# The bidirectional recurrence of a two-block transformer: preparation without GpSimd, two products per chunk in the chain

## The chip, the cores and the metric

One core of a Trainium2 chip. The metric is the device time of one execution, in microseconds, median of three runs. The kernel is written with a tile scheduler: the program lists instructions with their data, the scheduler decides in which order each engine gets them, and each engine works off its own queue in that order.

## The reference

Two blocks of two layers each over a sequence of 256 latent tokens (and 256 context tokens in the first block), width 1024. The first block's layers mix tokens in three ways at once, from one input projection: neighbourhood attention (512 columns), a bidirectional RWKV-7 recurrence (256 columns, 4 heads of 64) and a conformer convolution (256 columns). Layer 0 then has a feed-forward part, layer 1 a mixture of 8 experts of which each token takes two. The second block has block attention, spatial gating, a convolution and a feed-forward part. The recurrence is what the change is about:

```python
def _rwkv7_scan(r, w, k, v, z, b):
    def step(S, inp):
        r_t, w_t, k_t, v_t, z_t, b_t = inp
        s_z = jnp.einsum('ghvk,ghk->ghv', S, z_t)
        S = S * w_t[:, :, None, :] + s_z[..., None] * b_t[:, :, None, :] + v_t[..., None] * k_t[:, :, None, :]
        return S, jnp.einsum('ghvk,ghk->ghv', S, r_t)
    _, y = lax.scan(step, jnp.zeros((G, H, dh, dh), jnp.float32), (r, w, k, v, z, b))
    return y
...
    kk = kk * lax.rsqrt(jnp.sum(kk * kk, axis=-1, keepdims=True) + 1e-12)
...
        a = jax.nn.sigmoid(a0[d] + ad @ a2[d])
        kd = heads(k * (1.0 + (a - 1.0) * k_a))
        per_dir.append((heads(decay), kd, kk * heads(a), g))
```

z is −kk, b is kk·a, w the decay; the second direction runs over the reversed tokens. T is 512 (context, then latent). Layer 1 needs only the latent tokens' outputs.

## The kernel before

Weights are read from HBM as float32 and split into a high part (`wh`, a cast on ScalarE, L182) and a low part (`wl`, a subtraction, L183, on VectorE or GpSimd); each projection is three matmuls. `mixer()` builds one layer's mixing from generators: `prep` (p), `conv` (x), `gram` (g), `inverse` (i), `near` (n: projections of q, k and v of the neighbourhood attention), `chain` (c), `attend` (a), `taps` (t) and a few more. The string SEQ[layer] (L51 to L54) gives the order in which their steps are written down, a letter a step. For x and n the letter's case sets the engine of `wl`: lower case GpSimd, upper case VectorE. Each generator has PSUM banks of its own by tag: three for the recurrence's preparation, gram and inverse, four for near, one each for the chain's two directions.

The recurrence is done in 8 chunks of 64 tokens. The index `dh` is direction and pair of heads (four values, called heads here); the two heads of a pair lie in the partition halves 0 to 63 and 64 to 127.

- `prep`, per dh: ee and aa are sigmoids (a tanh on ScalarE, L519, and an affine pass on GpSimd, L520). A scan over ee (L624) gives cs, two exponentials the decays LAM and il (L626, L627). kd (L629, L630) and `ka` (L631, GpSimd) are multiplied by il into BK: two products 64x512 on VectorE and two on GpSimd (the loop of L632, products L634 and L635). kkn and r times LAM are ZR (L636, L637). `sqk` (L639) is the operand of the bonus.
- `gram`: masked products of BK and ZR give S for all chunks.
- `inverse`: of the triangular part, first on VectorE a solve of 32x32 blocks by rows (transposes Ad, L686; products and sums, L696 and L698, into Xi), then transposes of Xi into TD and TN (L704, L706), then on TensorE products with TN, copied to Gs, and with Gs, copied into TD.
- `near` multiplies the tokens with the q, k and v weights: 192 matmuls of 512 columns and 192 of 256 columns (for v) in layer 0, half of q in layer 1. They write PSUM tiles, and ScalarE copies these to q, k and v.
- `chain`: per chunk `ready` turns v (identity products, L776 copies them into UV) and BK (transposes, L785 copies them, scaled, into BT). Then S·UV and ZR·PP are summed and copied to RH (L802), TD·RH is copied into UV (L810), BT·UV and the state PP make the next PP (L821 to L824). Last comes the output py (L835 copies it into ZR).

Every matmul is written at L154, every transpose at L158; the profile tells them apart by tile: `psprep`, `psgram`, `psinv`, `psnap` (near), `pschain`.

## Time and profile before

| | |
|---|---|
| runs | 2874.79, 2882.23, 2890.8 us; median 2882.23 |
| the profiled execution | 2886.99 us, its span 2885.2 us |
| TensorE busy | 2750.6 us, 95% of the span; granted clock 0.965 on average |
| VectorE, ScalarE, GpSimd busy | 1988.4 (69%), 1468.3 (51%), 348.5 us (12%) |

The first block's two layers take some 2,300 us of the span, 1,060 of them the experts. In layer 0 the preparation of the recurrence starts at 96.7 us, gram ends at 169.8, inverse and near projections at 260.4, the chain (with attention between) at 361.9. In layer 1 the same points are about 940, 1009, 1071 and 1165. Times are read from the span's start. A row of the timeline is an instruction, or a few of a kind (xN); what stands in brackets is the engine's idle time before it, and the instruction that ended it. A busy time of TensorE counts overlapping matmuls once; rows overlap, so that the distance of two starts is what one costs. The clock column is the granted clock of TensorE, 1.00 being 2.4 GHz.

### The profile page before, as it was taken

The page shows a single profiled execution, that of the slowest core. Times are in us where ns is not written, and L with a number is a line of the kernel's source. Part 1 is how long each engine was busy: PE and PEld are TensorE (multiplying, and loading weights), DVE is VectorE, ACT ScalarE, POOL GpSimd, SP SyncE. Part 2 cuts the span into 40 slices and gives each one's busy share as a digit, 9 for nine tenths or more (in the row PEclk, how much of TensorE's full clock was granted, in tenths as well). Part 3 has the DMA queues.
Part 4 walks back from the last instruction along what each step waited for, and adds up shares of the span by engine and source line. Part 5 has one row for each costly group of instructions (what it writes and reads, how often), then busy time and mean ns, then how long its engine had stood idle before and what let it go on. Part 6 is the DMA issues. An engine that isn't in the chain of part 4 may idle for free. (4 is left out here: it accounts for less than half of the span.)

```text
span 2885.2 us, 42860 instructions
## 1 busy us (share of the span) xinstructions
PE 2750.6 (95%) x17006; PEld 2257.8 (78%) x17006; DVE 1988.4 (69%) x2753; ACT 1468.3 (51%) x2032; POOL 348.5 (12%) x256
## 2 busy tenths in 40 slices
PE   6998999999998879999989999999999999999999
PEld 4677656778886766677867777778777889998999
DVE  4685474322225796488878888888889868856784
ACT  3313243322224332477757777767777646644563
POOL 1420012211001610100000000000000221301120
PEclk9898799999999998999999999999999999999999
DMA  6122155333333224579988999899989835553453
GB/s 227 51 74 74 52 150 193 96 123 94 97 99 105 81 88 140 173 293 352 319 321 325 322 353 344 328 338 362 337 325 349 307 114 175 183 183 117 161 184 109
DMA packets 108098, 585.77 MB, mean 203 GB/s; under 512 B 12657, under 2 KB 19825, under 8 KB 54129
## 3 DMA queue, kind: packets, MB, share of 16 engines
q1 hardware_dynamic: 107888, 582.95, 57.5%
q8 instruction: 136, 2.23, 0.3%
q14 instruction: 74, 0.60, 0.1%
HBM read 580.80 MB, written 2.10 MB: 202 GB/s over the span
## 5 line engine op out<-in xcount | busy, mean ns | idle before, releaser
L183 DVE TENSOR_TENSOR wl<-wr,wh 128x1024 fp32r<-128x1024 f32 x978 | 1169.5, 1225 | 477.9 <-ACT wh L182 465.6
L182 ACT CAST wh<-wr 128x1024 fp32r<-128x1024 f32 x992 | 1003.8, 1044 | 681.1 <-PE psffn L154 193.2
L154 PE MATMUL psmoe<-wh,xH 128*128 128x512 f32 x896 | 354.9, 397 | 3.4 <-ACT wh L182 3.4
L154 PE MATMUL psmoe<-wl,xH 128*128 128x512 f32 x896 | 356.2, 398 | 1.0 <-DVE wl L183 0.7
L154 PE MATMUL psmoe<-wh,xL 128*128 128x512 f32 x896 | 355.5, 397 | 0.0
L154 PEld LDWEIGHTS psmoe<-wl,xH 128*128 128x128 f32 x896 | 168.3, 188 | 45.6 <-DVE wl L183 6.5
L154 PEld LDWEIGHTS psmoe<-wh,xH 128*128 128x128 f32 x896 | 168.4, 188 | 44.4 <-ACT wh L182 5.0
L154 PE MATMUL pssf<-oh,wl 128*128 128x256 f32 x704 | 199.5, 284 | 0.0
L154 PE MATMUL pssf<-ohT,wh 128*128 128x256 f32 x704 | 199.2, 284 | 0.0
L154 PEld LDWEIGHTS psmoe<-wh,xL 128*128 128x128 f32 x896 | 168.4, 188 | 39.1
L154 PE MATMUL pssf<-oh,wh 128*128 128x256 f32 x704 | 198.9, 284 | 0.0
L154 PE MATMUL psmoe<-wh,aL 128*128 128x512 f32 x448 | 178.3, 398 | 2.0 <-DVE aL L183 2.0
L154 PE MATMUL psmoe<-wh,aH 128*128 128x512 f32 x448 | 175.6, 397 | 2.5 <-ACT aH L182 2.5
L154 PE MATMUL psmoe<-wl,aH 128*128 128x512 f32 x448 | 163.3, 400 | 0.0
L1551 POOL TENSOR_SCALAR x<-x,fin 128x256 f32<-128x256 f32 x8 | 12.2, 1542 | 1057.5 <-DMA wr<-w_in 1057.3
L154 PE MATMUL psffn<-h2L,wh 128*128 128x512 f32 x352 | 138.7, 394 | 1.3 <-POOL h2L L257 1.3
L154 PE MATMUL psffn<-h2H,wh 128*128 128x512 f32 x352 | 138.2, 395 | 1.0 <-ACT h2H L256 1.0
L154 PE MATMUL psffn<-h2H,wl 128*128 128x512 f32 x352 | 137.5, 392 | 0.0
L154 PEld LDWEIGHTS pssf<-oh,wl 128*128 128x128 f32 x704 | 135.2, 192 | 0.0
L154 PEld LDWEIGHTS pssf<-ohT,wh 128*128 128x128 f32 x704 | 135.1, 192 | 0.0
L154 PEld LDWEIGHTS pssf<-oh,wh 128*128 128x128 f32 x704 | 135.0, 192 | 0.0
L154 PEld LDWEIGHTS psmoe<-wh,aL 128*128 128x128 f32 x448 | 84.2, 188 | 24.4 <-DVE aL L183 4.4
(476 smaller groups left out, 5624.6 us busy)
## 6 DMA issues: line engine op xcount, KB each, us to landing
wr<-moe_w_gate SPq DMA_DIRECT2D x112, 1024.0 KB, 7.0
wr<-moe_w_up SPq DMA_DIRECT2D x112, 1024.0 KB, 6.6
wr<-moe_w_down SPq DMA_DIRECT2D x112, 1024.0 KB, 7.0
wm<-mod_w SPq DMA_DIRECT2D x96, 512.0 KB, 4.3
wr<-f_up SPq DMA_DIRECT2D x44, 1024.0 KB, 4.9
wr<-w_in SPq DMA_DIRECT2D x52, 512.0 KB, 3.8
wr<-w_in SPq DMA_DIRECT2D x16, 1024.0 KB, 5.0
wr<-f_down SPq DMA_DIRECT2D x16, 1024.0 KB, 5.0
```

The lines of the kernel that those rows point to most:

```text
L154: i = self.nc.tensor.matmul(out, lhsT, rhs, start=start, stop=stop, **kw)
L182: self.nc.scalar.copy(H, src)
L183: (eng or self.nc.vector).tensor_sub(L, src, H.bitcast(F32))
L1551: nc.gpsimd.tensor_scalar(x[:, k], x[:, k], fin[:, k:k + 1], None, op0=ALU.mult)
```

## The change

In `prep` GpSimd is left with little. The sigmoid's affine pass goes to ScalarE; aa stays a tanh, and the constants (`oka`, `hka`, and `kkh`, half of kkn) make up for it; kd's affine pass goes to ScalarE, `ka` to VectorE, and so do all four products of BK. In SEQ[0] the conv's steps are lower case (their L parts go to GpSimd), one step of near's becomes lower case, and chain steps stand between those of near's v part.

In the recurrence a new function `turned()` stands at the start of `inverse`. It turns v of all chunks (into UV, which has two places: the LAM tile, and a new one), multiplies S with them, scales BK of seven chunks in place by the decay of the chunk, transposes it and writes it back, and turns ZR by identity products. Behind each half of the inverse, TD multiplies the turned ZR. A chunk of the chain then has two dependent products: ZR·PP, added to a TD·UV that is already in the bank, copied into UV; and BK·UV, added to the scaled state. The solve's Ad, Xi and Gs no longer have a pool of their own but lie in the tile of near's v, and `self.after` asks that the second part of near's v comes behind the last TD·ZR.

```diff
-SEQ = [("pppppgggXXggggggggggggginNnniNNcactcccttatcatt...
+SEQ = [("pppppgggxxggggggggggggginNnnicNccNactcttatcatt...
...
         def sigm(dst, src, **kw):
             nc.scalar.activation(dst, src, AF.Tanh, scale=0.5, **kw)
-            nc.gpsimd.tensor_scalar(dst, dst, 0.5, 0.5, op0=ALU.mult, op1=ALU.add)
+            nc.scalar.activation(dst, dst, AF.Copy, scale=0.5, bias=0.5)
...
+                kkh = PA.tile([128, 2, 512], F32, name=self.nm("kkh"))
+                nc.scalar.activation(kkh, kkn, AF.Copy, scale=0.5)
...
-                        sigm(aa, p2, bias=hw[:, 4 + dh:5 + dh])
+                        nc.scalar.activation(aa, p2, AF.Tanh, scale=0.5, bias=hw[:, 4 + dh:5 + dh])
...
-                        nc.vector.tensor_scalar(kd, aa, P("ka", hp), oka[:, hp:hp + 1], op0=ALU.mult, op1=ALU.add)
+                        nc.scalar.activation(kd, aa, AF.Identity, scale=hka[:, hp:hp + 1], bias=oka[:, hp:hp + 1])
                         nc.vector.tensor_mul(kd, kd, kx[:, hp])
-                        nc.gpsimd.tensor_mul(ka, aa, kkn[:, hp])
-                        for ab, eng in ((0, nc.vector), (1, nc.gpsimd)):
+                        nc.vector.scalar_tensor_tensor(ka, aa, 1.0, kkh[:, hp], op0=ALU.add, op1=ALU.mult)
+                        for ab in range(2):
                             o = slice(64 * ab, 64 * ab + 64)
-                            eng.tensor_tensor(o4(BK[o, dh, :, 1 - ab]), rv(ka[o], d), il4[o], ALU.mult)
-                            eng.tensor_tensor(o4(BK[o, dh, :, ab]), rv(kd[o], d), il4[o], ALU.mult)
+                            nc.vector.tensor_tensor(o4(BK[o, dh, :, 1 - ab]), rv(ka[o], d), il4[o], ALU.mult)
+                            nc.vector.tensor_tensor(o4(BK[o, dh, :, ab]), rv(kd[o], d), il4[o], ALU.mult)
...
+        def turned():
+            nc.vector.tensor_copy(lam, LAM[:, :, :, 64])
+            UV = LAM[:, :, :, 0:64], PC.tile([128, 4, 8, 64], F32, name=self.nm("UV"))
+            for c in range(8):
+                pv = self.ps((128, 2, 2, 2, 64))
...
+                            self.mm(pv[o, 0, d, hp], (vr if d else vv)[o, hp, c * 64:c * 64 + 64], self.ident[o, o], True, True, chain=pv)
...
+                    nc.scalar.copy(UV[ab][o, :, c], pv[o, 0].rearrange("p d h t -> p (d h) t"))
...
+                            self.mm(pv[r, 1, d, hp], S[o, ab, (2 * d + hp) * 8 + c, 0:64], UV[ab][o, 2 * d + hp, c], True, True, chain=pv)
...
+                    nc.scalar.copy(UV[ab][r, :, c], pv[r, 1].rearrange("p d h t -> p (d h) t"))
...
+                    nc.scalar.activation(b, b, AF.Copy, scale=lam[:, dh, c:c + 1])
+                    self.tp(pb[:, dh].rearrange("p a t -> p (a t)"), b, self.ident, chain=pb)
+                for ab in range(2):
+                    nc.scalar.activation(BK[:, :, c, ab], pb[:, :, ab], AF.Copy, scale=self.sg[:, ab:ab + 1])
+            for dh in range(4):
...
+                        self.mm(pz[r, c], ZR[o, dh, c + 1, 0], self.ident[o, o], True, True, chain=pz)
+                nc.scalar.copy(ZR[:, dh, 1:, 0], pz)
         def inverse():
+            turned()
...
-                Ad = PI.tile([128, 32, 32], F32, name=self.nm("Ad"), tag="Ad")
-                Xi = PI.tile([128, 32, 32], F32, name=self.nm("Xi"))
+                Ad, Xi = [v[:, 2 * i:2 * i + 2].rearrange("p a b -> p (a b)").rearrange("p (a b) -> p a b", a=32) for i in range(2)]
...
-                Gs = PI.tile([128, 32, 32], F32, name=self.nm("Gs"), tag="Ad")
+                Gs = Ad
...
+                    for dh in range(2 * uh, 2 * uh + 2):
...
+                                inverted = self.mm(pz[o, c], ZR[r, dh, c + 1, 0], TD[r, dh * 8 + c + 1], True, True, chain=pz)
+                        nc.vector.tensor_copy(ZR[:, dh, 1:, 0], pz)
...
         def near():
+                if inverted is not None:
+                    self.after = inverted.ins.name
...
+            def own(d, c):
+                W = self.ps((128, 2, 2, 64), tag=f"c{d}")
...
+                            self.mm(W[o, 0, hp], BK[:, 2 * d + hp, c - 1, ab], UV[ab][:, 2 * d + hp, c - 1], True, True, chain=W)
...
+                        self.mm(W[r, 1, hp], TD[r, (2 * d + hp) * 8 + c], UV[ab][r, 2 * d + hp, c], hp == 0, c == 0 and hp == 1, chain=W)
```

What it moves. VectorE in layer 0, preparation of the second of the four heads, before (cs is the scan, `sqk` the bonus operand):

```order
L624 SCALAR_TENSOR_TENSOR cs_802<-msk_730,ee_800 128x256 x2
L629 TENSOR_SCALAR kd_804<-aa_801,prm_71,oka_208 128x512
L629 TENSOR_SCALAR kd_837<-aa_834,prm_71,oka_208 128x512
L630 TENSOR_TENSOR kd_804<-kd_804,kx_472 128x512
L634 TENSOR_TENSOR BK_462<-ka_805,il_803 64x8x64
L635 TENSOR_TENSOR BK_462<-kd_804,il_803 64x8x64
L636 TENSOR_TENSOR ZR_458<-kkn_729,LAM_463 128x8x64
L637 TENSOR_TENSOR ZR_458<-rr_471,LAM_463 128x8x64
L639 SCALAR_TENSOR_TENSOR sqk_827<-rr_471,prm_71,kd_804 128x512
```

and now:

```order
L633 SCALAR_TENSOR_TENSOR cs_805<-msk_732,ee_803 128x256 x2
L639 TENSOR_TENSOR kd_807<-kd_807,kx_474 128x512
L640 SCALAR_TENSOR_TENSOR ka_808<-aa_804,kkh_768 128x512
L645 TENSOR_TENSOR ZR_460<-kkn_731,LAM_465 128x8x64
L643 TENSOR_TENSOR BK_464<-ka_808,il_806 64x8x64
L644 TENSOR_TENSOR BK_464<-kd_807,il_806 64x8x64
L643 TENSOR_TENSOR BK_464<-ka_808,il_806 64x8x64
L644 TENSOR_TENSOR BK_464<-kd_807,il_806 64x8x64
L646 TENSOR_TENSOR ZR_460<-rr_473,LAM_465 128x8x64
L648 SCALAR_TENSOR_TENSOR sqk_829<-rr_473,prm_71,kd_807 128x512
```

Two BK rows and the `ka` row have come in; the two kd rows with scalars are gone.

TensorE in layer 0 at the end of gram, before:

```order
L154 MATMUL psgram_1120<-ZR_458,BK_462 128x128 x4
L154 MATMUL psgram_1126<-ZR_458,BK_462 128x128 x4
L154 MATMUL psnap_1277<-hH_235,wh_1267 128x512
L154 MATMUL psnap_1277<-hL_236,wh_1267 128x512
L154 MATMUL psnap_1277<-hH_235,wl_1268 128x512
```

and now, where vv and vr are v and its reverse, `cst` the identity, LAM and UV the two places of the turned v:

```order
L155 MATMUL psnap_1590<-hL_238,wh_1580 128x512
L155 MATMUL psnap_1590<-hH_237,wl_1581 128x512
L155 MATMUL psinv_1170<-cst,vv_221 64x64 x4
L155 MATMUL psinv_1170<-cst,vr_222 64x64 x3
L155 MATMUL psinv_1138<-cst,vv_221 64x64 x4
L155 MATMUL psinv_1138<-cst,vr_222 64x64 x4
L155 MATMUL psinv_1170<-cst,vr_222 64x64
L155 MATMUL psinv_1202<-cst,vv_221 64x64 x4
L155 MATMUL psinv_1202<-cst,vr_222 64x64 x4
L155 MATMUL psnap_1590<-hH_237,wh_1580 128x512
L155 MATMUL psinv_1138<-LAM_465,S_905 64x64
L155 MATMUL psinv_1138<-UV_1137,S_905 64x64
```

Before, 192 matmuls of near's follow the gram products without a break. Now the products of `turned` come first, with 11 of near's between them, and the other 181 behind. Ahead of the last 52 gram products, 30 conv products stood behind the last `sqk`; now 13 do.

TensorE in layer 1, at the first products with TN, before (here 146 products of near's v part stand ahead of them):

```order
L154 MATMUL psnap_7997<-wl_7985,hH_6500 128x256
L154 MATMUL psnap_7994<-wh_7990,hH_6500 128x256
L154 MATMUL psnap_7994<-wh_7990,hL_6501 128x256
L154 MATMUL psinv_7597<-TN_7589,S_7357 32x32
L154 MATMUL psinv_7667<-TN_7589,S_7357 32x32
```

and now, at the last products of TD and ZR, behind which 147 of near's v part stand:

```order
L155 MATMUL psnap_8362<-wl_8358,hH_6609 128x256
L155 MATMUL psinv_8188<-TD_7465,ZR_6675 64x64 x14
L155 MATMUL psinv_8204<-TD_7465,ZR_6675 64x64 x14
L155 MATMUL psnap_8361<-wh_8351,hH_6609 128x256
L155 MATMUL psnap_8361<-wh_8351,hL_6610 128x256
```

The v products that ran ahead of TN now run behind the inverse. Ahead of the gram of layer 1, 25 near products of 512 columns stood between the last lora products and the gram's last groups; now 6 do.

## Rows read from the trace of the kernel before

**Rows 1.** The page, part 1: busy time, share of the span, instructions.
```profile
PE 2750.6 (95%) x17006; PEld 2257.8 (78%) x17006; DVE 1988.4 (69%) x2753; ACT 1468.3 (51%) x2032; POOL 348.5 (12%) x256
```

**Rows 2.** Windows: stretch, length; busy PE, PEld, DVE, ACT, POOL; clock, DMA share, GB/s.
```profile
96.70:169.80 73.10, 64.42 (x298) 46.97 (x296) 50.95 (x64) 16.27 (x24) 42.05 (x26) 0.77 0.14 44
169.80:260.40 90.60, 78.91 (x643) 69.45 (x642) 64.22 (x141) 23.02 (x35) 10.76 (x4) 0.89 0.20 65
260.40:361.90 101.50, 100.48 (x1042) 70.76 (x1044) 52.96 (x131) 30.13 (x74) 0.61 (x1) 0.80 0.20 63
220.00:240.00 20.00, 14.11 (x284) 13.39 (x285) 10.57 (x6) 4.61 (x8) 0.00 (x0) 0.52 0.16 54
940.00:1009.00 69.00, 57.50 (x390) 48.54 (x388) 53.99 (x69) 21.95 (x32) 44.24 (x26) 0.90 0.27 85
1009.00:1071.00 62.00, 46.48 (x524) 42.22 (x525) 57.52 (x134) 15.65 (x26) 12.64 (x5) 0.89 0.17 52
1230.00:2290.00 1060.00, 1026.87 (x4608) 823.32 (x4607) 911.08 (x915) 758.41 (x852) 1.72 (x3) 0.99 0.90 334
```

**Rows 3.** Timeline of TensorE: start, length, instruction, idle before it and releaser.
```profile
148.87 1.75 PE L154 MATMUL psprep<-cst,sqk 128*128 128x2 f32 x8 [4.96 <-DVE sqk L639]
...
160.01 9.84 PE L154 MATMUL psgram<-ZR,BK 64*128 64x128 f32 x104
...
226.10 3.62 PE L154 MATMUL psinv<-TN,S 32*32 32x32 f32 x126 [5.84 <-DVE TN L706]
...
1057.20 0.38 PE L154 MATMUL psinv<-TN,S 32*32 32x32 f32 x4 [14.34 <-DVE TN L706]
```

**Rows 4.** Timeline of VectorE in the first layer's preparation.
```profile
111.88 0.75 DVE L607 SCALAR_TENSOR_TENSOR kkn<-kx,prm,psprep 128x512 f32<-128x512 f32 x1 [4.19 <-PE psprep L158]
...
126.05 1.76 DVE L635 TENSOR_TENSOR BK<-kd,il 64x512 f32<-64x512 f32 x1
...
134.28 0.67 DVE L634 TENSOR_TENSOR BK<-ka,il 64x512 f32<-64x512 f32 x1
134.88 0.67 DVE L635 TENSOR_TENSOR BK<-kd,il 64x512 f32<-64x512 f32 x1
...
136.74 1.25 DVE L624 TENSOR_TENSOR_SCAN cs<-msk,ee 128x256 f32<-128x256 f32 x2
...
143.50 0.68 DVE L634 TENSOR_TENSOR BK<-ka,il 64x512 f32<-64x512 f32 x1 [3.79 <-POOL ka L631]
...
148.08 0.74 DVE L639 SCALAR_TENSOR_TENSOR sqk<-rr,prm,kd 128x512 f32<-128x512 f32 x1
```

**Rows 5.** Timeline of GpSimd in the same stretch.
```profile
134.04 6.82 POOL L634 TENSOR_TENSOR BK<-ka,il 64x512 f32<-64x512 f32 x1 [3.05 <-ACT il L627]
```

**Rows 6.** Timeline of TensorE in the first layer's chain.
```profile
260.38 0.45 PE L154 MATMUL pschain<-cst,vv 64*64 64x64 f32 x8
...
262.38 0.66 PE L158 MATMUL pschain<-cst,BK 128*128 128x128 f32 x4 [0.26 <-ACT UV L776]
262.97 0.68 PE L154 MATMUL pschain<-UV,S 64*64 64x64 f32 x16
```

**Rows 7.** ScalarE in that chain: two rows of its timeline, one group by line.
```profile
261.58 0.74 ACT L776 COPY UV<-pschain 64x256 f32<-64x256 f32 x2
...
263.89 0.84 ACT L785 ACTIVATE BT<-pschain,cst 128x256 f32<-128x256 f32 x2
...
L876 ACT COPY q<-psatt 128x128 f32<-128x128 f32 x3 | 0.8, 265 | 4.4 <-PE psatt L154 4.4
```

**Rows 8.** Timeline of TensorE, near products: first and last of 25, and of 40.
```profile
170.12 0.40 PE L154 MATMUL psnap<-hL,wh 128*128 128x512 f32 x1
...
175.58 0.39 PE L154 MATMUL psnap<-hL,wh 128*128 128x512 f32 x1
...
1038.04 0.28 PE L154 MATMUL psnap<-wh,hL 128*128 128x256 f32 x1
...
1042.59 0.28 PE L154 MATMUL psnap<-wh,hL 128*128 128x256 f32 x1
```

More of the change, by code (lines that the diff above doesn't have):

```diff
@@ L144, in __init__ @@
         self.last = {}
+        self.after = None
         self.n = 0
@@ L154, in mm @@
         i = self.nc.tensor.matmul(out, lhsT, rhs, start=start, stop=stop, **kw)
+        if self.after is not None:
+            self.tc.add_manual_dep(i.ins, self.after, NOSYNC, reason="the order of two stages")
+            self.after = None
         return self._chain(i, chain)
@@ L484, in mixer @@
         oka = P0.tile([128, 2], F32, name=self.nm("oka"))
-        nc.vector.tensor_scalar(oka, P("ka", 0, 2), -1.0, 1.0, op0=ALU.mult, op1=ALU.add)
+        hka = P0.tile([128, 2], F32, name=self.nm("hka"))
+        nc.vector.tensor_scalar(oka, P("ka", 0, 2), -0.5, 1.0, op0=ALU.mult, op1=ALU.add)
+        nc.vector.tensor_scalar(hka, P("ka", 0, 2), 0.5, None, op0=ALU.mult)
         hw = P0.tile([128, 74], F32, name=self.nm("hw"))
@@ new lines, in own @@
+            def own(d, c):
+                W = self.ps((128, 2, 2, 64), tag=f"c{d}")
+                if c:
+                    for hp in range(2):
+                        for ab, (o, r) in enumerate(halves):
+                            self.mm(W[o, 0, hp], BK[:, 2 * d + hp, c - 1, ab], UV[ab][:, 2 * d + hp, c - 1], True, True, chain=W)
+                for hp in range(2):
+                    for ab, (o, r) in enumerate(halves):
+                        self.mm(W[r, 1, hp], TD[r, (2 * d + hp) * 8 + c], UV[ab][r, 2 * d + hp, c], hp == 0, c == 0 and hp == 1, chain=W)
+                return W
@@ new lines, in chain @@
+            PP, LP = [None, None], [None, None]
+            W = [own(d, 0) for d in range(2)]
+            for c in range(8):
+                Pn = [None, None]
+                for d in range(2):
+                    if PP[d] is not None:
+                        for hp in range(2):
+                            for o, r in halves:
+                                self.mm(W[d][r, 1, hp], ZR[o, 2 * d + hp, c, 0], PP[d][o, hp], False, hp == 1, chain=W[d])
+                    for ab, (o, r) in enumerate(halves):
+                        nc.vector.tensor_copy(UV[ab][r, 2 * d:2 * d + 2, c], W[d][r, 1])
+                for d in range(2):
+                    if c == 7:
+                        break
+                    W[d] = own(d, c + 1)
+                    Pn[d] = PC.tile([128, 2, 64], F32, tag=f"PP{d}", name=self.nm("PP"), bufs=2)
+                    if LP[d] is None:
+                        nc.vector.tensor_copy(Pn[d], W[d][:, 0])
+                    else:
+                        nc.vector.tensor_add(Pn[d], W[d][:, 0], LP[d])
+                for d in range(2):
+                    if c < 6:
+                        LP[d] = PC.tile([128, 2, 64], F32, tag=f"LP{d}", name=self.nm("LP"))
+                        nc.vector.tensor_tensor(LP[d], Pn[d], lam[:, 2 * d:2 * d + 2, c + 1:c + 2].to_broadcast([128, 2, 64]), ALU.mult)
+                if need or c >= 4:
+                    py = self.ps((128, 2, 2, 64), tag="x")
+                    for d in range(2):
@@ L811, in chain @@
-                    for d in range(2):
-                        if c == 7:
-                            break
-                        pp = self.ps((128, 2, 64), tag=f"c{d}")
-                        for hp in range(2):
-                            for ab, (o, r) in enumerate(halves):
-                                self.mm(pp[o, hp], BT[:, d, hp, ab], UV[:, d, hp, ab], True, True, chain=pp)
-                        Pn[d] = PC.tile([128, 2, 64], F32, tag=f"PP{d}", name=self.nm("PP"))
-                        lam = LAM[:, 2 * d:2 * d + 2, c, 64:65].to_broadcast([128, 2, 64])
-                        if PP[d] is None:
-                            nc.vector.tensor_tensor(Pn[d], pp, lam, ALU.mult)
-                        else:
-                            nc.vector.tensor_add(Pn[d], pp, PP[d])
-                            nc.vector.tensor_tensor(Pn[d], Pn[d], lam, ALU.mult)
@@ L825, in chain @@
-                    nxt = ready(c + 1) if c < 7 else None
-                    if need or c >= 4:
-                        py = self.ps((128, 2, 2, 64), tag="x")
-                        for d in range(2):
-                            for hp in range(2):
-                                u = (2 * d + hp) * 8 + c
-                                for ab, (o, r) in enumerate(halves):
-                                    self.mm(py[o, d, hp], UV[:, d, hp, ab], S[:, ab, u, 64:128], True, PP[d] is None, chain=py)
-                                    if PP[d] is not None:
-                                        self.mm(py[o, d, hp], PP[d][o, hp], ZR[o, 2 * d + hp, c, 1], False, True, chain=py)
-                        nc.scalar.copy(ZR[:, :, c, 1], py.rearrange("p d h t -> p (d h) t"))
@@ L836, in chain @@
-                    PP = Pn
-                    if nxt:
-                        UV, BT = nxt
-                        yield
+                                    self.mm(py[o, d, hp], PP[d][o, hp], ZR[o, 2 * d + hp, c, 1], False, True, chain=py)
+                    nc.scalar.copy(ZR[:, :, c, 1], py.rearrange("p d h t -> p (d h) t"))
+                PP = Pn
+                if c < 7:
+                    yield
             SS.close()
```

68 lines of the change are left out of this document (27 added, 41 removed).

## The prediction

> **What bounds the kernel now.** I read the page's busy times first. TensorE is busy 95% of the span and VectorE 69% [rows 1], so nearly every stage is TensorE's, and time can come only from places where TensorE waits, from slow clock, or from less work on it. The table by stage [rows 2] shows where that is. The expert stage is full (1026.9 us busy of 1060), so what an earlier stage saves shortens the whole run. The stages that the change touches are not full. In the first layer preparation and gram take 73.1 us with 64.4 busy, inverse and near projections 90.6 with 78.9, the chain 101.5 with 100.5. In the second layer it is 69.0 with 57.5, and 62.0 with 46.5. Together TensorE idles there 48 us, and its granted clock is 0.77 to 0.90, between its two levels of 1.2 and 2.4 GHz.
>
> The timeline of TensorE says who ends those waits [rows 3]: in preparation the bonus operand `sqk` of VectorE (4.96 us), in the inverse the transposes TN of VectorE (5.84 us in the first layer, 14.34 us in the second). So VectorE is the clock of both stages. What makes it slow in preparation is in [rows 4]: a BK product that follows an undisturbed one begins 0.60 us after it (134.28 to 134.88), but lasts 1.76 us at 126.05, and once VectorE stands 3.79 us for GpSimd's `ka`. GpSimd pays too: one BK product of its own took 6.82 us [rows 5].
>
> **Preparation, first layer.** GpSimd loses the half-scalings of ee and aa, `ka` and two of four BK products per head. ScalarE takes the second pass of ee, the affine pass of kd and one halved kkn, some ten passes; it is busy 16.3 of 73.1 us [rows 2], so I cost them at nothing. Without that cover each pass would sit between lora product and scan. VectorE gains two BK products and `ka` per head and loses the affine pass. By starts in [rows 4]: per head one scan pair 1.25 us, seven products (kd, four BK, two ZR) at 0.60, two scalar-tensor-tensor passes at about 0.67 are 6.8 us; four heads and the kkn pass 27.8 us. The conv's L parts (`wl`) go from VectorE to GpSimd with the lower-case x. Four fall into this stretch, each of which may hold up a VectorE product by the 1.1 us between 0.67 and 1.76, or two of them, so I add 5 us: 32.8. Now it is 36.9 us, from 111.88 to 148.82 [rows 4]: 4.1 us less.
>
> The second part is order. Before, TensorE gets the last `sqk` at 148.87, done at 150.6, and then runs 30 conv products until gram goes on at 160.0 [rows 3]. In the new order 13 stand there; the other 17, at 9.4/30 = 0.31 us each, fill the earlier waits: 5.3 us. One `wl` less ahead of the first pass, 1 us. Sum 10.4; I take **−11**. Bounds: 64.4 us of TensorE work at the present clock leaves 8.7 to gain without a better clock; if only the VectorE part comes, −4; if the contention vanishes entirely, −15.
>
> **Preparation, second layer.** The same edits per head. Idle there is 11.5 us. In addition the new order leaves 6 of the 25 near products of 512 columns that now fill waits between lora and gram; 19 move behind the gram (they return below, at 4.3 us). They ran at the lower clock there, so they take up about 8 us. I take a third of the idle and these, **−12**, bounds −6 and −15.
>
> **Inverse and chain: what moves.** Per layer 64 products by the identity (vv, vr), 28 transposes of BK and 64 products S·V move from the chain into a new stretch `turned`, ahead of the inverse. A product is two records in the trace, so by [rows 6] they cost 64 × 0.11, 28 × 0.165 and 64 × 0.085: 17.2 us. New are 56 products that turn ZR (0.11 each as identity products, 6.2 us) and 56 TD·ZR (0.085, 4.8 us): **11.0 us more TensorE work per layer**. TD·RH and BT·UV keep their number under other names.
>
> `turned` is paced by ScalarE: per chunk four copies 64x256 (two pairs of 0.74), four in-place scalings of BK (128x128, 0.265) and two scaled copies (0.84) [rows 7], 3.4 us; seven chunks 23.7, the last chunk's copies 1.5, four copies of ZR at most 3.4: 28.5 us. TensorE has 23.4 us of work in it and the order puts about 11 near products (0.228 each [rows 8]) between: 2.6 us idle. Below 28.5 it cannot go with ScalarE as it is; above, if each round trip between the two engines is exposed, 52 (rival one). I take 28.5, as the chain before hides the same hand-overs.
>
> **First layer, after gram.** The remaining 181 near products take 41.2 us, so TensorE reaches TN 69.7 us after gram. VectorE has TN ready after 50 to 56 us (226.10 [rows 3] less 169.8), so both waits are gone. From 220 to 240 the clock was 0.52 with 14.1 us busy [rows 2], which at full clock is 7.3: 6.8 gained. Against 11.7 + 1.0 us of idle now: new work 11.0, idle in `turned` 2.6, hand-overs after each half's TD 1.6, together 15.2 − 12.7 − 6.8 = **−4**. Bounds −10 (no idle left) and +10. VectorE gains four copies of ZR and loses the RH copies; it is busy 53.0 of 101.5 us in the chain, so that costs nothing. ZR's copies must be out before the chain's second chunk; the v products stand between.
>
> **Second layer, after gram.** Here Ad, Xi and Gs lie in near's tile v. Before, 146 v products ran ahead of TN; now the copies into v must wait until Gs is read, and the order keeps 147 v products behind the last TD·ZR. TN is ready 48 us after gram; `turned` and the 81 near products that are left take 28.5 + 18.5 = 47, so 1 us of the 14.34 us wait stays. Then each half (TN, TD, TD·ZR and 20 to 25 v products at 0.117 [rows 8]) takes about 8 us, and v 17.2: the chain starts some 82 us after gram, not 62. The chain gets 17.2 us shorter. In sum: 11.0 new, 4.3 from the 19 moved products, 5.2 idle, less 15.5 idle now and 2 at the lower clock after the long wait: **+3**. Bounds −3 and +12.
>
> SP's queue and the DMAs keep their issues, except that Xi's constants now land in v; nothing else reads v by then.
>
> **Sum**: −11 − 4 − 12 + 3 = −24 us against the profiled execution, 2886.99 us (span 2885.2). The median of the three runs is 2882.23, 4.8 lower; I set the change against it: 2858.
>
> **Rivals.**
> *One, slower: `turned` becomes a chain of round trips.* All 28 BK scalings are in ScalarE's queue ahead of the first copy of V, behind the last gram mask, and the near products placed between are few. Exposed end to end, a chunk is 0.9 + 0.74 + 0.68 + 0.74 + 1.06 + 0.66 + 0.84 = 5.6 us, seven and the eighth 42, ZR 10: 52 us, 23 more than I take. First layer +23, second +21: −24 + 44 = +20, **2902**. It takes back the gain from 40 us on. For it: TensorE's queue is in order, and three banks serve all tiles. Against it: in the chain such hand-overs cost TensorE only 1.0 us of 101.5 [rows 2].
> *Two, preparation gains nothing:* VectorE, which ends the waits, takes over work. If the L parts on GpSimd disturb it as much as BK products did, what remains is two BK and `ka` per head, 4 × 1.9 = 7.5 us, less the affine passes (2) and the wait for GpSimd (3.8): +1 to +2 per layer in place of −11 and −12. Sum +2, **2884**. Against it: the 1.76 us beside 0.67. The Trainium skill, Perfetto Trace Analysis, section Optimizing Scalar/DVE Operations, advises to take work off a saturated VectorE and give it to ScalarE or even GpSimd, which is the reverse of this change; by that rule this rival is right, and the same section adds that shifting between VectorE and GpSimd might not help. The trace speaks for the rule in that VectorE ends the waits, and against it by the 6.82 us product.
> *Three, the clock comes back:* with fewer holes the first layer's preparation runs at 0.90 rather than 0.77 (64.4 to 55 us) and its chain at 0.89 rather than 0.80 (101.5 to 91): 19 more, **2839**. Against it: the chain had 1.0 us of idle and still 0.80.
>
> **How the numbers follow.** Forecast 0.56, rival one 0.17, two 0.14, three 0.13. Half a per cent, 14.4 us, is about what a measurement of this kernel can tell from no change. The forecast's terms, all at their bad bounds, would be past zero, so of its 0.56 I count 0.46 as faster by more than that and 0.10 as the same; rival three is faster, two the same; of rival one 0.06 is the same (`turned` half exposed, some 40 us) and 0.11 slower. Faster 0.59, same 0.30, slower 0.11. The range leaves a tenth on each side: 2832, where rival three meets the good bounds, to 2892, short of the full price of rival one.
>
> **What would show it.** Preparation: BK products of VectorE at 0.67 us throughout, few rows at 1.76 beside GpSimd's `wl`, and 60 to 64 us from 96.7 to the end of gram. `turned`: about 28 us from the last gram product to the near products that follow in a row, ScalarE nearly full in it. First layer: no wait for TN. Second: a wait for TN under 3 us, chain starting 80 us or more after gram, and 75 to 80 us long. Wrong would be a `turned` over 40 us, a TN wait in the first layer, or VectorE longer than 37 us from kkn to the last `sqk`.

## The result, and the profile after

The changed kernel takes 2907.84 us (median of 11 runs, 2896.58 to 2925.9), the kernel before 2882.23 (11 runs, 2874.79 to 2893.41). The ratio is 1.0098, 95% interval 1.0077 to 1.0119: slower by 28 us by the ratio (26 between the medians), where 24 us of gain were forecast. The profiled execution has a span of 2906.6 us against 2885.2.

TensorE's and ScalarE's busy times have grown, VectorE's and GpSimd's have fallen [rows 1]. The page, after:

```profile
PE 2792.9 (96%) x17454; PEld 2281.1 (78%) x17454; DVE 1961.6 (67%) x2745; ACT 1515.8 (52%) x2150; POOL 290.6 (10%) x216
```

Windows of TensorE's stages after, columns as in [rows 2]: projections ahead (layer 0), preparation with gram, inverse, chain, attention, then the first four of these in layer 1.

```profile
28.70:98.30 69.60, 67.80 (x307) 47.34 (x308) 33.84 (x41) 29.20 (x44) 14.33 (x13) 0.95 0.39 135
98.40:163.30 64.90, 58.09 (x298) 41.73 (x297) 49.40 (x70) 30.04 (x59) 18.20 (x9) 0.84 0.13 44
163.30:248.20 84.90, 79.67 (x992) 65.17 (x994) 53.87 (x141) 36.73 (x77) 9.61 (x4) 0.98 0.15 51
248.20:345.00 96.80, 96.80 (x883) 70.65 (x877) 41.72 (x98) 19.49 (x42) 0.00 (x0) 0.81 0.23 77
345.00:456.60 111.60, 104.90 (x634) 57.11 (x634) 67.68 (x153) 42.95 (x115) 22.89 (x21) 0.87 0.45 142
897.80:950.80 53.00, 50.54 (x242) 41.13 (x243) 29.45 (x36) 26.78 (x43) 11.99 (x12) 0.89 0.28 95
950.80:1019.10 68.30, 60.05 (x383) 52.59 (x382) 49.06 (x78) 37.47 (x69) 10.32 (x6) 0.80 0.22 70
1019.10:1100.00 80.90, 76.05 (x1048) 65.92 (x1047) 54.12 (x138) 35.58 (x77) 14.91 (x6) 0.94 0.15 47
1100.00:1176.20 76.20, 75.19 (x739) 44.56 (x739) 45.57 (x130) 15.68 (x37) 0.61 (x1) 0.84 0.52 160
```

The windows of before that [rows 2] lack or cut otherwise (chain, cut where its last product py ends, and the attention behind it; projections ahead in both layers; preparation with gram and chain of layer 1):

```profile
260.40:353.20 92.80, 91.78 (x1001) 65.54 (x1001) 49.00 (x122) 26.20 (x64) 0.00 (x0) 0.80 0.20 64
353.20:446.80 93.60, 89.59 (x620) 48.83 (x620) 59.12 (x135) 41.25 (x113) 24.56 (x21) 0.97 0.49 152
29.40:96.70 67.30, 65.24 (x308) 46.80 (x308) 34.99 (x42) 27.97 (x42) 13.29 (x14) 0.97 0.40 133
888.50:938.30 49.80, 48.34 (x240) 39.39 (x241) 30.09 (x36) 25.90 (x41) 12.54 (x14) 0.95 0.30 101
938.30:1009.10 70.80, 59.30 (x403) 50.34 (x402) 54.73 (x69) 23.56 (x34) 44.65 (x27) 0.90 0.26 82
1070.90:1154.80 83.90, 82.99 (x1032) 54.34 (x1031) 55.90 (x161) 26.43 (x65) 0.61 (x1) 0.91 0.52 158
```

The preparation is shorter, by 8.2 us in layer 0 and by 2.5 in layer 1. The stages behind it are longer in sum: inverse, chain and attention of layer 0 take 293.3 us against 277.0, inverse and chain of layer 1 157.1 against 145.7. The projections ahead, which the prediction did not look at, take 2.3 and 3.2 us more. In sum that is +22.5 us, about the 21.4 between the spans. The granted clock goes with it: the chain has 0.81, as before, but the attention behind it 0.87 instead of 0.97. Products of k and q in the attention show that level, one row of the timeline of TensorE after and one before:

```profile
346.94 2.07 PE L155 MATMUL psatt<-k,q 64*128 64x512 f32 x2
```
```profile
357.30 1.12 PE L154 MATMUL psatt<-k,q 64*128 64x512 f32 x2
```

Two products of the same shape take nearly twice as long in the row after, at 1.2 instead of 2.4 GHz.

### The profile page after: what moved, and what is told of

Its sections match the earlier page's. It is cut to its first block, busy times and chain, and to the rows that moved or that the text cites. A ratio compares the mean times of both kernels' runs of the same rounds, so it can differ in the third digit from the quotient of the medians.

```text
span 2906.6 us, 43820 instructions
## 1 busy us (share of the span) xinstructions
PE 2792.9 (96%) x17454; PEld 2281.1 (78%) x17454; DVE 1961.6 (67%) x2745; ACT 1515.8 (52%) x2150; POOL 290.6 (10%) x216
```

## The experiments

My theory was that the new products cost about what the change saves and that the rest is TensorE's clock. Rivals were the tile shared with v, the order of v, and the turning of ZR itself. Each ratio is to the kernel before, with its interval, from five rounds.

### The two parts alone

First, the kernel before with the new preparation and only the lower-case x of SEQ[0]; second, the changed kernel with the old preparation.

```diff
... (kkh, hka, the affine passes on ScalarE, ka and all BK products on VectorE, as in the change)
-SEQ = [("pppppgggXXggggggggggggginNnniNNcactcccttatcatt...
+SEQ = [("pppppgggxxggggggggggggginNnniNNcactcccttatcatt...
```

> The kernel before with the edits of the preparation alone (affine passes on ScalarE, ka and BK on VectorE, the conv's low parts on GpSimd); the recurrence is that of before. Theory A (the preparation gains, the recurrence part loses): the first layer's preparation and gram take about 65 us as in the changed kernel instead of 73, the second layer's about 68 instead of 71, the projections ahead of them up to 5 us longer; in sum 5 to 12 us faster than before, ratio 0.996 to 0.998. Theory B (the preparation itself loses, by the slower clock after a longer wait for sqk): no faster, 0 to 10 us slower, ratio 1.000 to 1.004.

Measured: 1.0006 (0.9981 to 1.0032).

> The changed kernel with the preparation of before (GpSimd back in it), everything else changed. Theory A: the loss is here, 25 to 40 us slower than before (ratio 1.009 to 1.014), slower than the changed kernel by what the preparation gains. Theory B: 10 to 20 us slower than before, faster than the changed kernel.

Measured: 1.0046 (1.0023 to 1.0068). So no gain of the preparation by itself is seen, and the recurrence costs 13 us by itself. The chain of layer 0 in the first of these kernels has the products of the chain before. The windows of that stage and of its inverse in layer 1:

```profile
254.30:332.90 78.60, 77.21 (x1001) 54.62 (x1000) 48.69 (x122) 26.20 (x64) 0.00 (x0) 1.00 0.24 75
986.50:1054.20 67.70, 51.88 (x539) 47.09 (x538) 59.25 (x134) 16.62 (x26) 14.39 (x6) 0.88 0.17 54
```

The chain takes 78.6 us at clock 1.00 where before took 92.8 at 0.80. So this stage can move by 14 us with nothing changed in it, and a small change can't be priced by such a stage of one execution.

### Without the new products

From the changed kernel the turning of ZR and TD·ZR are taken out (56 and 56 products per layer, with their copies; the chain then multiplies the unturned ZR). Then the same is taken out of the second kernel above.

```diff
-            for dh in range(4):
...
-                        self.mm(pz[r, c], ZR[o, dh, c + 1, 0], self.ident[o, o], True, True, chain=pz)
-                nc.scalar.copy(ZR[:, dh, 1:, 0], pz)
...
-                    for dh in range(2 * uh, 2 * uh + 2):
...
-                                inverted = self.mm(pz[o, c], ZR[r, dh, c + 1, 0], TD[r, dh * 8 + c + 1], True, True, chain=pz)
-                        nc.vector.tensor_copy(ZR[:, dh, 1:, 0], pz)
```

> The changed kernel without the 112 products per layer that are new in it (the turning of ZR by the identity, and TD times the turned ZR, with their eight copies per layer): the chain multiplies the unturned ZR, so the values differ from the reference, the chain's instructions stay. Theory A (TensorE is the bound after the change, new work adds its full time): 15 to 20 us faster than the changed kernel, ratio to before 1.002 to 1.005. Rival C (the new products lie in waits and cost nothing; the loss is elsewhere): within 5 us of the changed kernel, ratio to before 1.008 or more.

Measured: 1.0024 (1.0001 to 1.0047), 0.0074 less than with them, 21 us.

> The changed recurrence with the preparation of before and without the 112 new products per layer. If the parts add: 1.0046 less 0.0074, 0.997 of before (8 us faster), so that the new chain would pay if its turning were free. If the new products only cost beside the new preparation: 1.002 or more.

Measured: 1.0039 (1.0014 to 1.0065). That misses the 0.997 of adding parts and is the number of the second theory: 0.0007 less than with them. The windows of the inverse of layer 1 beside the old preparation, with the new products and without:

```profile
1001.30:1081.90 80.60, 70.21 (x1027) 61.39 (x1027) 55.61 (x138) 34.88 (x78) 12.05 (x5) 0.94 0.12 41
997.00:1071.20 74.20, 63.52 (x803) 55.65 (x803) 54.12 (x134) 32.78 (x74) 12.07 (x5) 0.91 0.14 44
```

The stage gets 6.4 us shorter without them, and that of layer 0 6.9 (84.2 to 77.3). Beside the new preparation it is 7.2 and 6.8. So in their own stages the products cost the same in both pairs, and the theory that they only cost beside the new preparation is not borne out there. But the chain of layer 0 has a clock of 0.81 to 1.00 in these four profiles, and the twelve runs of the last kernel lie between 2875 and 2913 us, so the question was left until the clock was under control.

### The tile, and the order of v

Ad, Xi and Gs of layer 1 in a pool of their own; the same with the order edge of that layer gone; and the changed kernel with the old order of chain and v in SEQ[0].

```diff
+if not need:
+    Ad = PI.tile([128, 32, 32], F32, name=self.nm("Ad"))
+    Xi = PI.tile([128, 32, 32], F32, name=self.nm("Xi"))
```
```diff
-if inverted is not None:
+if inverted is not None and need:
```
```diff
-SEQ = [("pppppgggxxggggggggggggginNnnicNccNactcttatcatt...
+SEQ = [("pppppgggxxggggggggggggginNnniNNcactcccttatcatt...
```

> The changed kernel with Ad, Xi and Gs of the second layer in a pool of their own instead of in near's tile v (the first layer has no room for it). Theory A: the second layer's TensorE idles only 4 us for TN, so that v products ahead of TN win at most that: 0 to 5 us faster than the changed kernel. Rival D (the tie to v is the loss, since the chain of layer 1 starts 81 us after gram and not 62): 12 to 19 us faster than the changed kernel, ratio to before 1.002 to 1.006.

Measured: 1.0078 (1.0051 to 1.0105).

> The changed kernel, with Ad, Xi and Gs of the second layer in a pool of their own and without the order edge that holds the second part of near's v behind the last product of TD and ZR there: nothing but data now orders v against the inverse. Theory A (TensorE is the bound there): 0 to 6 us faster than the changed kernel, though the chain of layer 1 starts earlier. Rival D (the tie to v is the loss): 12 to 19 us faster.

Measured: 1.0075 (1.0047 to 1.0104).

> The changed kernel with the middle of SEQ[0] as before: all of near's v part in layer 0 stands ahead of the chain, not between its first chunks. Theory A (TensorE is the bound; order inside a full stretch is worth little): within 6 us of the changed kernel. Rival F (the attention's late start in layer 0, 289 instead of 255 to 261 us, is the loss): 8 to 16 us faster, since the chain again runs beside the attention from its first chunk.

Measured: 1.0108 (1.0082 to 1.0134). None differs from the changed kernel by more than the intervals allow. The stages of inverse and chain in layer 1 are 80.7 and 76.3 us with the own pool and 80.9 and 76.2 without. But these two kernels did not try the order itself: in both, TensorE still runs all 192 products of near's v behind the first product with TN, and still waits 3.2 us for it. That the shared tile costs little there follows from the idle time alone: the inverse of layer 1 has 4.9 us of it after the change (80.9 less 76.05), and an earlier v could fill no more than that.

The kernel with the own pool shows something else. Its edit leaves layer 0 alone, and the products of its chain there stand in the same order as in the changed kernel, where the stage took 96.8 us at clock 0.81:

```profile
249.60:334.50 84.90, 84.47 (x881) 63.71 (x875) 41.67 (x98) 19.47 (x42) 0.00 (x0) 0.96 0.26 88
```

### Turning twice

```diff
-self.mm(pz[r, c], ZR[o, dh, c + 1, 0], self.ident[o, o], True, True, chain=pz)
+for _ in range(2):
+    self.mm(pz[r, c], ZR[o, dh, c + 1, 0], self.ident[o, o], True, True, chain=pz)
```

> The changed kernel with each of the 56 identity products that turn ZR in a layer done twice. Theory A (TensorE is the bound): the time of 112 such products, 0.036 us a record and two records a product, 8 us slower than the changed kernel, ratio to before 1.011 to 1.014. Rival C (they lie in a wait for ScalarE or VectorE): within 2 us of the changed kernel.

Measured: 1.0063 (1.0039 to 1.0086), a miss for both theories: more work, and 0.0035 faster than the changed kernel. Its profile has the chain of layer 0 at clock 1.00, 81.9 us, where the changed kernel has 96.8 at 0.81. So I looked for what lowers the clock in the chain.

### The order of py

py adds S·UV, a product over 128 rows, and ZR·PP, one over 64, and the code writes them in turn. Timeline of TensorE, before:

```profile
289.10 0.33 PE L154 MATMUL pschain<-S,UV 128*64 128x64 f32 x2
289.36 0.32 PE L154 MATMUL pschain<-ZR,PP 64*64 64x64 f32 x2
289.61 0.33 PE L154 MATMUL pschain<-S,UV 128*64 128x64 f32 x2
```

A pair of records (one product) starts 0.25 us after the last pair, 0.13 us a record. The edit writes the 8 products over 128 rows first and then the 8 over 64. With the order it also changes the flags that open and close a sum: one group per half instead of one per tile. It is made to the kernel before, to the changed one, and to the kernel with the new preparation alone:

```diff
-self.mm(py[o, d, hp], UV..., S[:, ab, u, 64:128], True, PP[d] is None, chain=py)
+self.mm(py[o, d, hp], UV..., S[:, ab, u, 64:128], d == 0 and hp == 0, PP[d] is None and d == 1 and hp == 1, chain=py)
+for d in range(2):
+    for hp in range(2):
+        for ab, (o, r) in enumerate(halves):
             if PP[d] is not None:
-                self.mm(py[o, d, hp], PP[d][o, hp], ZR[o, 2 * d + hp, c, 1], False, True, chain=py)
+                self.mm(py[o, d, hp], PP[d][o, hp], ZR[o, 2 * d + hp, c, 1], False, d == 1 and hp == 1, chain=py)
```

> The kernel before, with the chain's output products py in another order: first the eight products UV times S of a chunk (128 rows), then the eight PP times ZR (64 rows), as one accumulation group per half instead of one per tile; now the two kinds alternate, a pair of records starts 0.26 us after the last one. Theory A (in the chain TensorE is the bound, and the alternation costs 0.13 us a record where products of one kind cost 0.045): 370 records in both layers at 0.08 to 0.09 less, 25 to 33 us faster than before, ratio 0.988 to 0.992. Rival (the price is the shape's, or the chain waits for something else): within 5 us of before.

Measured: 0.9843 (0.9817 to 0.9869), 2838.78 us. It is faster than both kernels, and by more than the 25 to 33 us that I had expected. Timeline of TensorE, then windows of chain and attention (layer 0) and chain (layer 1):

```profile
290.49 0.69 PE L154 MATMUL pschain<-S,UV 128*64 128x64 f32 x16
291.10 0.51 PE L154 MATMUL pschain<-ZR,PP 64*64 64x64 f32 x10
```
```profile
260.50:320.10 59.60, 58.08 (x1004) 41.59 (x1004) 48.52 (x122) 26.88 (x65) 0.00 (x0) 1.00 0.28 92
320.10:415.40 95.30, 91.41 (x616) 48.91 (x617) 59.22 (x135) 40.61 (x112) 24.54 (x21) 0.95 0.48 152
1040.20:1107.10 66.90, 65.36 (x1032) 42.49 (x1031) 54.97 (x160) 26.46 (x65) 0.88 (x1) 1.00 0.62 192
```

16 records now take 0.61 us, 0.038 each. The chain of layer 0 takes 59.6 us. Against the 78.6 of the same products at the same clock, 19 us are the edit at an even clock, and the other 14 of the 33 to the profile before are clock. Three more rows of the same trace tell whether the flags, or a sum that is added to right behind its first part, could be the price instead of the row counts:

```profile
299.54 0.33 PE L154 MATMUL pschain<-UV,S 64*64 64x64 f32 x4
299.66 0.33 PE L154 MATMUL pschain<-PP,ZR 64*64 64x64 f32 x4
303.20 0.69 PE L154 MATMUL pschain<-UV,BT 128*64 128x64 f32 x16
```

The first two are S·UV and ZR·PP of RH, which alternate too, the second adding to the tile that the first has just written, but both run over 64 rows: 0.03 us a record. The third is BT·UV over 128 rows, every product a group of its own: the next row starts at 303.82, 0.039 us a record. So neither shows a price by itself, and the alternation of row counts is what is left.

> The changed kernel with py in that other order. Theory A: 25 to 33 us faster than the changed kernel, about the time of before (ratio 0.998 to 1.001); since py is the same in both kernels, the distance of changed to before stays 20 to 30 us when both have the new order. Rival E (the change's chain of two products is bound by its round trips, which the alternating py now hides): 0 to 15 us faster than the changed kernel.

Measured: 0.991 (0.9888 to 0.9932), 0.0188 less than the changed kernel; that too is more than I had expected.

> The preparation's edits alone plus py in the other order. If the preparation's edits are worth nothing by themselves (as the run of them alone, ratio 1.0006, says): the same as the kernel before with py reordered, within 6 us. If they were hidden by something in the chain: 8 to 15 us faster than that.

Measured: 0.9868 (0.9846 to 0.9891). The clock of the chain is 1.00 in both layers in all eight profiles of kernels with this order (these and those below). The other ten have 0.73 to 1.00 in layer 0, three of them 1.00, and 0.84 to 0.94 in layer 1. With the chain's clock even, the change costs 0.9910 − 0.9843 = 0.0067, and its preparation still gains nothing (+0.0025).

> The recurrence's part of the change alone (preparation of before) with py reordered. If the extra loss of both parts together (0.0098 against 0.0006 and 0.0046) sits in the clock after the chain: with py reordered the parts add, 10 to 16 us slower than the kernel before with py reordered and within 5 us of the changed kernel with py reordered (ratio to before 0.988 to 0.991). If the parts really work against each other: 0.987 or less.

Measured: 0.9902 (0.988 to 0.9924), so the new recurrence alone costs 0.0059; with the preparation's 0.0025 that is 0.0084, and the intervals allow it to be the 0.0067. The parts add up as far as these runs can tell.

> The changed kernel without its 112 new products per layer (as in the run without them) and with py in the other order. Theory A (the new products are what separates the two kernels): within 6 us of the kernel before with py reordered, ratio to before 0.982 to 0.987. Rival G (the new chain costs something by itself, which py's alternation hid): 10 us or more slower than that, ratio 0.988 or more.

Measured: 0.9846 (0.9823 to 0.9869), 0.0064 below the changed kernel with this order (18 us), as the first pair above said; here the chain has the same clock in both. The windows of its two inverse stages, 78.1 and 73.6 us, against 85.1 and 80.7 with the new products:

```profile
165.30:243.40 78.10, 69.03 (x754) 55.10 (x753) 52.32 (x138) 34.84 (x73) 9.63 (x4) 0.96 0.18 55
974.00:1047.60 73.60, 67.34 (x825) 58.75 (x824) 52.88 (x134) 33.64 (x73) 14.87 (x6) 0.94 0.16 52
```

> The changed kernel with py reordered and the identity products that turn ZR done twice. If new TensorE work adds its time where the chain keeps its clock: 4 us a layer, 6 to 10 us slower than the changed kernel with py reordered (ratio to before 0.993 to 0.995). Rival C (they lie in waits): within 3 us of it, 0.991 or less.

Measured: 0.9926 (0.9899 to 0.9952), 0.0016 above, some 5 us for 112 more products, between what the two theories expected. The intervals would also allow none. The sign is no longer that of the first run, which fits that its miss was the chain's clock; more than that is not shown.

### The two-column constant

`hka`, half of ka's weights in two columns, is a VectorE instruction of the new preparation. With it, in layer 1, a weight cast (`wh`) of the projections ahead stands behind the last cast of the normalized tokens in ScalarE's queue, and without it ahead of that cast; in layer 0 the casts stand in the same order either way. The edit gives it to GpSimd, in the two kernels with the new order of py:

```diff
-nc.vector.tensor_scalar(hka, P("ka", 0, 2), 0.5, None, op0=ALU.mult)
+nc.gpsimd.tensor_scalar(hka, P("ka", 0, 2), 0.5, None, op0=ALU.mult)
```

> The preparation's edits with py reordered, and the two-column product hka on GpSimd instead of VectorE, which puts the third weight cast of the projections back ahead of the last token cast in both layers. If the order of those casts takes the preparation's gain: the projections ahead of the preparation 67 and 50 us as before instead of 70 and 53, in sum 5 us faster than the same kernel with hka on VectorE (ratio to before 0.984 to 0.986). Rival: 0 to 2 us.

Measured: 0.985 (0.9823 to 0.9877), 0.0018 lower.

> The changed kernel with py reordered and hka on GpSimd. Same theory: 5 us faster than the changed kernel with py reordered (ratio to before 0.988 to 0.990), still 10 to 16 us slower than the kernel before with py reordered.

Measured: 0.9877 (0.9853 to 0.99), 0.0033 lower. Windows of chain and attention in layer 0, then projections ahead and inverse in layer 1:

```profile
250.10:314.50 64.40, 63.61 (x883) 49.20 (x879) 41.78 (x99) 19.56 (x42) 0.00 (x0) 1.00 0.35 116
314.50:413.40 98.90, 90.96 (x633) 48.60 (x632) 67.45 (x153) 42.58 (x115) 23.51 (x21) 1.00 0.53 160
856.00:905.50 49.50, 47.84 (x241) 39.31 (x242) 30.08 (x36) 26.66 (x43) 10.97 (x12) 0.96 0.29 101
974.00:1054.70 80.70, 75.86 (x1049) 65.73 (x1048) 53.91 (x138) 35.56 (x77) 14.92 (x6) 0.94 0.15 47
```

The projections ahead in layer 1 are back at 49.5 us, as before (49.8), instead of 53.0; those of layer 0 are not (70.3). So some 3 us of the 0.0033 (9 us) have a place. Most of the 10 us between the two profiles lies in the stretch from the last expert product to the end, which no edit touches, here with `hka` on VectorE and on GpSimd:

```profile
2242.20:2852.10 609.90, 599.88 (x4823) 583.81 (x4822) 432.45 (x650) 314.00 (x494) 122.55 (x87) 0.98 0.44 152
2240.70:2842.10 601.40, 593.81 (x4822) 578.01 (x4822) 432.82 (x650) 313.96 (x494) 123.47 (x87) 0.99 0.45 154
```

In the eighteen profiles that stretch takes 600 to 613 us. The same edit without the new order of py was not tried.

Of the 0.0098 the differences between kernels give three parts of like size: 0.0034 (10 us) is left with the new order of py and `hka` on GpSimd, 0.0033 lies between `hka` on VectorE and on GpSimd, and 0.0031 is what the old order of py costs the changed kernel more than the kernel before. Each is about as large as its own uncertainty, so that none is shown by itself; their sum is.

## Why the prediction was wrong

**Preparation, layer 0, −11: −8.2 measured.** VectorE's part held; how TensorE gained from it was only in part as I had it. Timelines of VectorE and GpSimd after:

```profile
113.82 0.75 DVE L614 SCALAR_TENSOR_TENSOR kkn<-kx,prm,psprep 128x512 f32<-128x512 f32 x1 [3.29 <-PE psprep L162]
...
125.44 0.68 DVE L643 TENSOR_TENSOR BK<-ka,il 64x512 f32<-64x512 f32 x1
126.05 0.68 DVE L644 TENSOR_TENSOR BK<-kd,il 64x512 f32<-64x512 f32 x1
...
137.65 2.84 DVE L648 SCALAR_TENSOR_TENSOR sqk<-rr,prm,kd 128x512 f32<-128x512 f32 x1
...
146.59 0.74 DVE L648 SCALAR_TENSOR_TENSOR sqk<-rr,prm,kd 128x512 f32<-128x512 f32 x1
```
```profile
137.28 2.66 POOL L187 TENSOR_TENSOR wl<-wr,wh 128x1024 fp32r<-128x1024 f32 x1 [4.52 <-ACT wh L186]
```

The BK products run at 0.68 us where [rows 4] had 1.76, and from kkn to the end of the last `sqk` it is 33.5 us (32.8 forecast, 36.9 before). Two passes stand 2.8 us each beside a `wl` of GpSimd (one pair is shown), some 4 us in all, where I had counted four and added 5. The Trainium skill, SBUF — State Buffer, section SBUF: two separate sides, says that VectorE and GpSimd share one pair of ports as an exclusive lock. The two rows agree: `sqk` ends 0.55 us after `wl`.

TensorE's idle time fell only from 8.7 to 6.8 us. The other 6.3 us are busy time, 64.4 to 58.1 for the same 298 records, as the clock rose from 0.77 to 0.84. I had put the gain into idle time, and the clock into rival three; that the number came near is in part luck.

**Preparation, layer 1, −12: −2.5 measured. This is the first step that failed,** as I put it: "I take a third of the idle and these", the 19 moved near products at 8 us. The third of the idle time came: it fell from 11.5 to 8.3 us. The 8 us did not. The near products left, and the inverse takes them back (with the new preparation alone it grows from 61.8 to 67.7 us), but TensorE's busy time in the preparation went from 59.3 to 60.1 us all the same, since the clock fell from 0.90 to 0.80. With fewer products to fill in, TensorE waits 5.96 us for the last `sqk`, and then gram runs at half clock. Timeline of TensorE after, then before:

```profile
998.44 1.01 PE L155 MATMUL psprep<-cst,sqk 128*128 128x2 f32 x4 [5.96 <-DVE sqk L648]
...
1000.72 18.43 PE L155 MATMUL psgram<-ZR,BK 64*128 64x128 f32 x104
```
```profile
986.39 1.01 PE L154 MATMUL psprep<-cst,sqk 128*128 128x2 f32 x4 [1.85 <-DVE sqk L639]
...
999.22 9.84 PE L154 MATMUL psgram<-ZR,BK 64*128 64x128 f32 x104
```

In all thirteen profiles with the new preparation this gram runs at a clock of 0.50, and the stage at 0.79 or 0.80; in all five with the old it runs at 1.00, and the stage at 0.88 to 0.93. Before, the near products stand between the wait and gram, and the clock rises while they run: they start 0.43 us apart at 994.9 and 0.23 at 996.6. So I read the products that the prediction saw as work at a lower clock as what brought gram to the higher one. No run moved them alone.

**Left out: the projections ahead.** +2.3 and +3.2 us. In layer 1 it goes with the order of casts: with `hka` on GpSimd it is gone. In layer 0 the cause is open: the casts stand as before, and kernels with the old preparation have 67.2 to 69.2 us there, those with the new 68.2 to 70.3. I priced what the change does inside its stages, and not what the scheduler makes of one more instruction ahead of them.

**Inverse.** `turned` is no chain of round trips: ScalarE's last copy of ZR ends at 186.4, 23 us after gram (28.5 forecast), in layer 1 24 us. It is shorter than forecast because only 4 of the 28 scalings of BK are left when gram ends. Rows of ScalarE's timeline, its last copies in layer 0, and a group of its instructions from 163 to 196 us by line:

```profile
183.82 0.95 ACT L732 COPY ZR<-psinv 128x448 f32<-128x448 f32 x2
185.05 0.53 ACT L732 COPY ZR<-psinv 128x448 f32<-128x448 f32 x1 [0.27 <-PE psinv L155]
185.87 0.54 ACT L732 COPY ZR<-psinv 128x448 f32<-128x448 f32 x1 [0.28 <-PE psinv L155]
```
```profile
L721 ACT ACTIVATE BK<-BK,lam 128x128 f32<-128x128 f32 x4 | 1.3, 387 | 0.0
```

TensorE reaches TN without a wait in layer 0, 70.5 us after gram (69.7 forecast), and in layer 1 waits 3.2 us for it:

```profile
233.76 1.20 PE L155 MATMUL psinv<-TN,S 32*32 32x32 f32 x64
...
1061.25 0.22 PE L155 MATMUL psinv<-TN,S 32*32 32x32 f32 x2 [3.18 <-DVE TN L764]
```

The chain of layer 1 starts 80.9 us after gram (82 forecast). Rival one falls with this.

**Layer 0 after gram, −4: +16.3 measured, the second step that failed.** Up to the end of the chain the account nearly held: inverse and chain take 1.7 us less (181.7 against 183.4), and their idle time fell from 12.7 to 5.2 us, where I had left 4.2. The loss is in the attention behind them, which I left out of the account: +18.0 us, 2.7 of them idle and 15.3 busy, at a clock of 0.87 instead of 0.97. The 6.8 us of clock that I booked as a gain were gained in the inverse (0.98 after, 0.89 before) and lost behind the chain. With the order of py changed in both kernels and `hka` on GpSimd, the three stages take 85.0, 64.4 and 98.9 us against 90.6, 59.6 and 95.3: +2.8, inside the bounds of −10 to +10. (The attention's clock is 1.00 and 0.95 there, so that the new work costs a few us more than this.) So a little of the loss comes from work that finds too little idle time, and most of the size from clock.

**Layer 1 after gram, +3: +11.4 measured,** and 80.7 + 56.8 against 61.6 + 66.9, +9.0, with the chain's clock even. Here a size was off: the new products cost 7 us in this stage and not 11.0, but the chain got only 10.1 us shorter (66.9 to 56.8), not 17.2. I had priced the moved work by the lengths of rows [rows 6], which overlap; by starts, eight records of the identity products after take 0.28 us (165.36 to 165.64), 0.07 a product and not 0.11. Both sums are inside the bounds.

**The rivals.** Two, that the preparation gains nothing, came true in its number (1.0006 alone), though not by its mechanism: VectorE did get shorter. The Trainium skill, Perfetto Trace Analysis, section Optimizing Scalar/DVE Operations, advises to take work off a saturated VectorE. VectorE here took BK and ka over, gave affine passes and `wl` away, and its stretch went from 36.9 to 33.5 us. So the trace does not bear out the ground on which the prediction called this rival right by that rule; that the kernel gained nothing lies with TensorE. Three, that the clock comes back with fewer holes, came in part in the first layer's preparation (0.84, not 0.90) and not in its chain: there it takes the order of py. The prediction's own sign, that the chain had 0.80 with 1.0 us of idle, pointed there and was used only against the rival.

**The signs.** None of the three signs of being wrong came: `turned` stayed under 40 us, TensorE had no wait for TN in the first layer, and VectorE stayed under 37 us. All three watch the mechanism that I had worked out, and none the clock or the stages outside the account, where the forecast failed.

**What stays open.** Six profiles of kernels with the new preparation, the new recurrence and the old order of py have the attention of layer 0 at 0.85 to 0.92; with the old preparation and that order it is 0.97 to 1.00, and with the new preparation and the old chain 0.99. Why the two together lower it isn't settled; with py reordered it is 0.98 to 1.00 for both together, but for one kernel (0.93). Nor was v of layer 1 ever put ahead of TN in the changed kernel, or the flags of py changed without its order.

## What to carry to other kernels

Before idle time of the bounding engine is counted as a gain, count the work that the change puts on that engine, through all stages up to the next full one, and ask whether products that look like filler hold its clock up. Read the timeline of a stage that is full and at a low clock for alternating shapes of matmuls: sorting them was worth 1.6% here with the same products, more than the whole change cost. A change that adds even a two-column instruction to a scheduled program may reorder a stage that it never touches, so compare all stages. And look at a stage that no edit touches, to see how far two profiles differ by themselves.

## What the hardware showed unexpectedly

- A matmul over 128 rows written in turn with one over 64 took 0.13 us a record, sorted 0.038, both with 64 columns. The Trainium skill, TensorEngine Tiling (Array Packing), section Tiling Modes, says that a change of the tiling mode drains TensorE, and lists 64 rows and 128 rows as different modes. The measured difference agrees. The price here is 0.09 us a record.
- While such products alternate, TensorE counts as busy (91.8 of 92.8 us), and the granted clock can be low all the same: 0.73 to 1.00 in ten profiles of the chain of layer 0, and 0.84 to 0.94 in that of layer 1. With them sorted it is 1.00 in both layers in eight of eight. That the order of py is what lowers it is shown by this pairing; how it does so is not, nor why it doesn't in three of the ten.
- The same products took 78.6 us in one kernel's execution and 92.8 in another's, at clocks of 1.00 and 0.80, and 84.9 and 96.8 us in two kernels with the same layer 0.
